# Gated linear attention of a hybrid decoder layer: tiles turned by VectorE and DMA instead of TensorE, and the order of three queues written out

## Chip, cores, metric

One core of a Trainium2 chip. The metric is the device time of one launch in microseconds, taken as the median of the runs; beside it stands one profiled execution, whose trace is read below. An engine's queue runs its instructions in order; the five engines wait for one another through semaphores.

## What is computed

One layer of a hybrid decoder, for a prompt of 2048 tokens and for 64 sampled tokens (8 sequences of 8). D is 1024, the feed-forward width 4096, everything in float32. Cut to what matters here:

```
h    = rms_norm(x, g_mix_pre)
proj = h @ w_in            # -> q, k, v (window attention) | gq, gk, gv, gr, glr (GLA)
attn = sliding-window attention with sinks, rotary, 8 q heads, 2 kv heads, hd 64
log_a = log_sigmoid(glr @ w_gk2 + b_gk) / 16
# GLA: 4 heads, dk 64, dv 128
S_t = exp(log_a_t) * S_{t-1} + k_t v_t^T          # state, 64 x 128 for each head
o_t = (q_t / 8) S_t
o   = rms_norm(o, g_gla) * silu(gr)
mix = concat(attn, o) @ w_out
x   = x + rms_norm(mix, g_mix_post)
x   = x + rms_norm(relu(rms_norm(x) @ w_up)^2 @ w_down, g_ffn_post)
```

Outputs are both streams, the last 128 keys and values, and the GLA states.

## The kernel before

The prompt is 16 tiles of 128 tokens (i = 0 to 15); the sampled tokens are a seventeenth (NB). The stages follow one another: window attention, GLA, output projection, feed-forward (up, then down). Float32 products are made of three products of rounded halves (high by high, high by low, low by high). This document is about the GLA stage, from about 308 to 675 us of the trace.

**Fill.** The loop over the tiles (L1545) runs the generator `gla(i)`. Wherever `gla` yields a number n, the loop emits n products from the generator `fill`: the input projection of later tiles (`projecting`, tile `gproj`, 96 products of 128x384 for one tile of tokens in four chunks of columns), and at the end the first output projections (128x512). So TensorE's queue is written out by hand (`te` is an `InOrder`, which ties each instruction to the one before it on that engine): pieces of `gla`, and between them so many products. The numbers are G_FILL, G_FIRST_FILL and, inside `finish_out`, 44. ScalarE copies each finished chunk out of PSUM into `gp` (L656, two buffers, one for each tile of tokens).

**gla(i).** Queries and keys come out of the projection with tokens on partitions; the products within a tile need them with features on partitions. `qk_T` (L1106) turns four 128x128 squares on TensorE (tile `gqk`), VectorE copies the keys to `kt` (L1114), ScalarE the two halves of the queries to `qz` (L1116). The decays are worked into seven levels of a tree: `level_sums` (L1150) makes, at each level, exponentials of two running sums (ScalarE) and two sums (VectorE); `weighted` (L1129) multiplies them into keys (XK) and queries (XQ). `keys_decayed` (L1137) makes the keys for the state's update and turns them back, two squares on TensorE (tile `kdT`, in the same bank as the turn of the ranks, L1145). Then the products of the levels (tiles `gl`, `gh`), of the update (`ds`) and with the old state (`o`, `ds`), from which `put_level` (L1162) picks masked parts into AH; ScalarE and VectorE make AT of it, and four products of AT with the values finish the output. `finish_out` (L1178) squares, takes a power on GpSimd, scales by the gate, turns four squares on TensorE (tile `ogT`) and stores them (`mo`, L1207, L1208) as rows 4 to 7 of `mix_d`, from which the output projection loads its left operand (L1392). `decayed(i + 1)` and the level sums 0 to 2 of the next tile stand ahead of the level products of this one.

**Order.** TensorE's order is laid down. VectorE, ScalarE and SyncE take the GLA stage's work as a planner places it; some instructions are tied by `issue_after`. Between tiles, two generators share the stage: `sampled` (the seventeenth tile's GLA) during the first tiles and then `split_wo` (L1438), which loads the eight slices of w_out, splits each (ScalarE and VectorE, 128x1024) and stores the parts, one slice for each tile.

Of the kernel before, what the change touches and what calls it, by code (L numbers as in the profile page):

```python
# [12 lines left out]
F32 = mybir.dt.float32  # L13
# [62 lines left out]
G_FILL = (34, 14, 16, 8, 20)  # L76
G_FIRST_FILL = 66
# [75 lines left out]
def hybrid_step_kernel(ctx: ExitStack, tc: tile.TileContext, I, O):  # L153
# [19 lines left out]
    te, ac, dv = (InOrder(tc, engine) for engine in (nc.tensor, nc.scalar, nc.vector))  # L173
# [22 lines left out]
    wo_d = [dpool.tile([P, 2, D], F32, name=f"wo_d{k}") for k in range(KT)]  # L196
    sm_d = dpool.tile([P, NFC, 2, 2 * NS], F32, name="sm_d")
# [427 lines left out]
    def load_T(i, xT):  # L625
        for u in range(2):
            dst = xT[1][:, :, u * NS : (u + 1) * NS] if i == NB else xT[u]
            nc.sync.dma_start(f32(dst), xt_d[i][:, u])
        return xT
# [346 lines left out]
    def log_decays(i, z, t, gt, out):  # L976
        for g in range(2):
            te.matmul(z[:, g], wgk[:, i % 2, g * P : (g + 1) * P], gt[:, : z.shape[2]], start=True, stop=True)
        nc.scalar.activation(t, z, AF.Abs)
        nc.scalar.activation(t, t, AF.Exp, scale=-1.0)  # L980
        if out is not None:
            nc.scalar.activation(out, t, AF.Ln, bias=1.0)
        return z
# [54 lines left out]
    ogs, mos = places("og", [P, 4, P]), places("mo", [P, 4, P])  # L1038
    XK = sp.tile([P, NL, 2, P], F32, name="XK")
    XQ = sp.tile([P, NL, 2, 2, P // 2], F32, name="XQ")  # L1040
    sgs, prs = places("sg", [P, 512]), places("pr", [P, 256])
# [3 lines left out]
    kts = places("kt", [P, 2, P], 2)  # L1045
# [29 lines left out]
    def decays(i, n, before, kind="d"):  # L1075
# [7 lines left out]
        if i:  # L1083
# [5 lines left out]
        nc.vector.scalar_tensor_tensor(before, z, 0.0, t, op0=ALU.min, op1=ALU.subtract)  # L1089

    def gate(i, gp, n):

        gr = gp[:n, 1024:1536]
        t = next(sgs) if n == P else s_sg
        nc.scalar.activation(t[:n], gr, AF.Abs)
        nc.scalar.activation(t[:n], t[:n], AF.Exp, scale=-1.0)
        nc.scalar.activation(t[:n], t[:n], AF.Ln, bias=1.0)
        nc.vector.scalar_tensor_tensor(t[:n], gr, 0.0, t[:n], op0=ALU.min, op1=ALU.subtract)
        nc.scalar.activation(t[:n], t[:n], AF.Exp)
        engine = nc.vector if i in (0, NB) else nc.gpsimd  # L1100
# [3 lines left out]
        return t  # L1104

    def qk_T(i, gp, n, kind="d"):  # L1106
# [6 lines left out]
        kt, q = (next(kts), qz) if n == P else (s_kt, s_qz)  # L1113
        nc.vector.tensor_copy(kt, pt[:, :, 0, :])  # L1114
        for r, rr in enumerate(half_of):
            nc.scalar.activation(q[rr, r], pt[rr, :, 1, :], AF.Copy, scale=0.125)  # L1116
        return kt
# [11 lines left out]
    def weighted(xk, xq, dec, kt, q, l, b):  # L1129

        dl, dr = (pairs(dec[:, l], b, s) for s in range(2))
        if l:
            nc.vector.tensor_tensor(pairs(xk[:, l], b, 0), dl, pairs(kt, b, 0), op=ALU.mult)
        out = xq[:, l].rearrange("p r g (m b) -> p r (g m) b", b=b)
        nc.vector.tensor_tensor(out, dr.unsqueeze(1).to_broadcast(list(out.shape)), pairs(q, b, 1), op=ALU.mult)

    def keys_decayed(after, kt, kdT, n, kind, kd, pair=0):  # L1137

        nc.scalar.activation(kdT, after, AF.Exp, scale=1.0 / 16)
        nc.vector.tensor_tensor(kdT, kdT, kt, op=ALU.mult)  # L1140
        yield
        pk = bank([P, 3, P], kind, f"kdT_{n}")
        for g in range(2):
            te.transpose(pk[:n, g, :], kdT[:, g, :], ident)
        ranks = ranks_T(pair, pk[:, 2]) if pair else None  # L1145
        nc.scalar.activation(kd[:n], pk[:n, :2].rearrange("p g k -> p (g k)"), AF.Copy)
        if pair:
            nc.scalar.activation(glrT[pair % 2], ranks, AF.Copy)

    def level_sums(before, after, dec, l, b):  # L1150

        left, right = halves(dec[:, l], b)
        (bl, br), al = halves(before, b), halves(after, b)[0]
        nc.scalar.activation(right, br, AF.Exp, scale=1.0 / 16)
        if l:
            nc.scalar.activation(left, al, AF.Exp, scale=1.0 / 16)
        nc.vector.tensor_tensor(al, al, br[..., b - 1 :].to_broadcast(list(al.shape)), op=ALU.add)
        nc.vector.tensor_tensor(br, br, bl[..., b - 1 :].to_broadcast(list(br.shape)), op=ALU.add)  # L1160

    def put_level(at, gm, mk, b):  # L1162
# [3 lines left out]
        nc.vector.copy_predicated(dst, m, gm.rearrange("p h (m b) -> p h m b", b=b))  # L1166

    def put_diagonal(i, at, gp, n):

        pr = next(prs)  # L1170
        with tc.issue_after(put[0].ins) if 0 < i < NB else nullcontext():
            nc.vector.scalar_tensor_tensor(pr[:n], gp[:n, 0:256], 0.125, gp[:n, 256:512], op0=ALU.mult, op1=ALU.mult)
        dg = sp.tile([P, 4], F32, tag="dg", name=f"dg_{i}", bufs=2)
        nc.vector.tensor_reduce(dg[:n], pr[:n].rearrange("p (h d) -> p h d", h=4), op=ALU.add, axis=AX.X)
        shape = [n, 4, HD]
        nc.vector.copy_predicated(at, dmsk[:n].unsqueeze(1).to_broadcast(shape), dg[:n].unsqueeze(2).to_broadcast(shape))

    def finish_out(i, og_src, sg, n, kind):  # L1178

        ssq = sp.tile([P, 4], F32, tag="ossq", name=f"ossq_{i}", bufs=2)  # L1180
        junk = sp.tile([P, P], mybir.dt.bfloat16, tag="ojunk", name=f"ojunk_{i}", bufs=1)
        for h in range(4):
            nc.scalar.activation(junk[:n], og_src(h), AF.Square, accum_out=ssq[:n, h : h + 1])
        rs = sp.tile([P, 4], F32, tag="ors", name=f"ors_{i}", bufs=2)
        rsqrt_mean(sp, rs[:n], ssq[:n], n, P, 4)
# [4 lines left out]
        for h in range(4):  # L1190
            with tc.issue_after(put[0].ins) if i == NB else nullcontext():
                nc.vector.scalar_tensor_tensor(
                    og[:n, h, :], og_src(h), rs[:n, h : h + 1], sg[:n, h * P : (h + 1) * P],
                    op0=ALU.mult, op1=ALU.mult,
                )
        for _ in range(S_WAIT[0] if i == NB else 1):
            yield 44, True
# [3 lines left out]
        if i == NB - 1:  # L1201
            hi, lo = late_mix
            nc.vector.tensor_copy(hi, pt)
            nc.vector.tensor_tensor(lo, pt, f32(hi), op=ALU.subtract)
        else:
            mo = next(mos)
            nc.scalar.activation(mo[:, :, :n], pt[:, :, :n], AF.Copy)  # L1207
            nc.sync.dma_start(mix_d[i][:, 4:8, :], mo[:, :, :n])  # L1208

    def decayed(i):  # L1210

        before, after = next(befores), next(afters)
        yield from decays(i, P, before, "d" if i else "b")
# [3 lines left out]
    def gla(i, gp, og=iter(())):  # L1217
# [4 lines left out]
        before, after = pre.pop(i)  # L1222
        next(og, None)
        kt = qk_T(i, gp, P, "c")
        dec = next(decs)
        following = decayed(i + 1) if i < NB - 1 else iter(())
        yield G_FILL[0] + 3 * (i == 1) if i else G_FIRST_FILL, True
        deque(og, 0)
        put_diagonal(i, AH, gp, P)
        for l, b in enumerate(LEVELS):  # L1230
            if l < 3 or i == 0:
                level_sums(before, after, dec, l, b)
            else:
                with tc.issue_after(put[0].ins):
                    level_sums(before, after, dec, l, b)
            if l == NL - 1:
                kd = next(kds)
                pair = i // 2 + 1 if i % 2 == 0 and i < NB - 2 else 0
                turned = keys_decayed(after, kt, next(kdTs), P, "e", kd, pair)
                nc.scalar.activation(dec[:, NL], before, AF.Exp, scale=1.0 / 16)  # L1240
            weighted(XK, XQ, dec, kt, qz, l, b)
        next(turned)
# [1209 lines left out]
```

## Time and profile before

| | |
|---|---|
| median of 3 runs | 2150.69 us (2150.44 to 2151.86) |
| the profiled execution | 2150.7 us, of it the span of the trace 2148.9 us |
| granted TensorE clock | 0.999 of full speed |
| TensorE busy | 99% of the span |
| VectorE, ScalarE, GpSimd busy | 71%, 57%, 12% |
| moved by DMA | 411.55 MB in 241323 packets |

Busy time of TensorE is modelled from pipelined instructions, each of which lasts longer than the distance to the next. How long a piece of its queue takes is therefore read from the start of the piece to the start of what follows it. The "mean ns" of an instruction of the other engines is its own duration; neighbours can overlap by some tens of ns.

### The profile page before, as it was taken

The page shows a single profiled execution, that of the slowest core. Times are in us where ns is not written, and L with a number is a line of the kernel's source. Part 1 is how long each engine was busy: PE and PEld are TensorE (multiplying, and loading weights), DVE is VectorE, ACT ScalarE, POOL GpSimd, SP SyncE. Part 2 cuts the span into 40 slices and gives each one's busy share as a digit, 9 for nine tenths or more (in the row PEclk, how much of TensorE's full clock was granted, in tenths as well). Part 3 has the DMA queues.
Part 4 walks back from the last instruction along what each step waited for, and adds up shares of the span by engine and source line. Part 5 has one row for each costly group of instructions (what it writes and reads, how often), then busy time and mean ns, then how long its engine had stood idle before and what let it go on. Part 6 is the DMA issues. An engine that isn't in the chain of part 4 may idle for free.

```text
span 2148.9 us, 34602 instructions
## 1 busy us (share of the span) xinstructions
PE 2137.8 (99%) x11974; PEld 1853.1 (86%) x11974; DVE 1530.2 (71%) x3200; ACT 1215.7 (57%) x2627; POOL 261.7 (12%) x422
## 2 busy tenths in 40 slices
PE   9999999999999999999999999999999999999998
PEld 9999999999998888888888888888888888888887
DVE  7999868778875666988887555557776666555566
ACT  7999867566664444655555544345444445544454
POOL 4676511111211110000000000000000000000000
PEclk9999999999999999999999999999999999999999
DMA  7444341243437567777886777668544443766685
GB/s 244 157 145 149 100 118 46 85 144 117 154 112 259 186 221 240 250 261 266 264 276 219 257 240 225 211 201 274 172 171 162 152 161 121 261 202 193 194 274 176
DMA packets 241323, 411.55 MB, mean 192 GB/s; under 512 B 24876, under 2 KB 143132, under 8 KB 237036
## 3 DMA queue, kind: packets, MB, share of 16 engines
q1 hardware_dynamic: 240988, 409.08, 57.6%
q8 instruction: 94, 1.54, 0.3%
q14 instruction: 81, 0.66, 0.1%
q10 hardware_dynamic: 160, 0.27, 0.0%
HBM read 265.82 MB, written 143.99 MB: 191 GB/s over the span
## 4 chain that ended last, share of the span: by engine, by line
PE 92%; DVE 3%; ACT 2%; DMA 1%; issue 1%; POOL 0%; SPq 0%; DVEq 0%; ACTq 0%; POOLq 0%
PE dn L142 28%; PE gproj L142 11%; PE uc L142 8%; PE uX L142 8%; PE out L1432 7%; PE proj L142 6%; PE ue L142 4%; PE ud L142 4%; PE ub L142 4%; PE dsam L142 1%; PE sc L142 1%; PE pT L142 1%; PE sam L142 1%; PE av L142 1%; PE out L142 1%
## 5 line engine op out<-in xcount | busy, mean ns | idle before, releaser
L142 PE MATMUL dn<-o0t,o0s 128*128 128x512 f32 x888 | 345.4, 389 | 0.6 <-DVE f L2090 0.6
L142 PE MATMUL dn<-o1t,o0s 128*128 128x512 f32 x888 | 345.7, 389 | 0.0
L142 PE MATMUL dn<-o0t,o1s 128*128 128x512 f32 x888 | 345.6, 389 | 0.0
L2076 DVE TENSOR_TENSOR o1s<-rs,o0s 128x512 fp32r<-128x512 f32 x224 | 154.5, 691 | 221.5 <-ACT o0s L2075 219.2
L2075 ACT ACTIVATE o0s<-rs 128x512 fp32r<-128x512 f32 x224 | 141.2, 631 | 291.4 <-PE dn L142 255.6
L142 PE MATMUL gproj<-wg,gxh 128*128 128x384 f32 x1024 | 271.1, 341 | 0.0
L142 PEld LDWEIGHTS dn<-o0t,o0s 128*128 128x128 f32 x888 | 166.8, 188 | 37.1 <-DVE f L2090 1.0
L142 ACT ACTIVATE st<-st 128x512 f32<-128x512 f32 x224 | 141.1, 630 | 100.5 <-DVE st L142 95.6
L142 PEld LDWEIGHTS dn<-o1t,o0s 128*128 128x128 f32 x888 | 166.7, 188 | 35.6 <-DVE o1t L2076 0.3
L142 PEld LDWEIGHTS dn<-o0t,o1s 128*128 128x128 f32 x888 | 166.7, 188 | 34.6
L142 PE MATMUL uc<-H,s 128*128 128x512 f32 x768 | 186.5, 391 | 0.1
L142 PEld LDWEIGHTS gproj<-wg,gxh 128*128 128x128 f32 x1024 | 183.8, 188 | 2.4 <-issue 1.9
L142 PE MATMUL gproj<-wg,gxl 128*128 128x384 f32 x576 | 185.9, 340 | 0.0
L142 PE MATMUL uX<-H,w 128*128 128x512 f32 x768 | 185.3, 390 | 0.0
L142 PEld LDWEIGHTS uX<-H,w 128*128 128x128 f32 x768 | 144.0, 188 | 30.4
L142 PEld LDWEIGHTS uc<-H,s 128*128 128x128 f32 x768 | 143.0, 188 | 30.6 <-ACT st L142 0.3
L1432 PE MATMUL out<-wo,mt 128*128 128x512 f32 x680 | 158.6, 392 | 0.0
L218 POOL TENSOR_TENSOR frs<-rs_v,half 128x1 f32<-128x1 f32 (+1 forms) x13 | 12.2, 944 | 1198.5 <-DVE rs_v L216 1198.5
L2076 DVE TENSOR_TENSOR o1t<-rt,o0t 128x512 fp32r<-128x512 f32 x222 | 151.9, 685 | 4.8 <-ACT o0t L2075 4.8
L1432 PEld LDWEIGHTS out<-wo,mt 128*128 128x128 f32 x680 | 126.5, 188 | 26.1
L2075 ACT ACTIVATE o0t<-rt 128x512 fp32r<-128x512 f32 x222 | 137.0, 619 | 8.8 <-DMA rt<-t_d 6.6
L142 DVE TENSOR_TENSOR st<-st 128x512 f32<-128x512 f32 x160 | 110.6, 692 | 31.4 <-ACT st L142 27.1
(444 smaller groups left out, 4314.8 us busy)
## 6 DMA issues: line engine op xcount, KB each, us to landing
s_d<-st SPq DMA_DIRECT2D x32, 1792.0 KB, 8.3
rs<-s_d SPq DMA_DIRECT2D x224, 256.0 KB, 3.6
raw<-in_w_up SPq DMA_DIRECT2D x64, 512.0 KB, 5.0
rt<-t_d SPq DMA_DIRECT2D x128, 256.0 KB, 3.9
rt<-in_w_down SPq DMA_DIRECT2D x96, 256.0 KB, 3.2
t<-in_w_down SPq DMA_DIRECT2D x64, 256.0 KB, 3.8
t_d<-t SPq DMA_DIRECT2D x32, 512.0 KB, 5.5
h_d<-ht SPq DMA_DIRECT2D x8, 1280.0 KB, 7.9
```

The source lines that it names most:

```text
L142: ins = call(*a, **k)
L218: return nc.gpsimd.tensor_tensor(out, v[:n], e, op=ALU.pow)
L1432: te.matmul(banks[c], x, w[:, c * 512 : (c + 1) * 512], start=k + u == 0, stop=k == KT - 1 and u == len(products) - 1,)
L2075: high = nc.scalar.activation(hi, raw, AF.Copy)
L2076: low = nc.vector.tensor_tensor(lo, raw, f32(hi), op=ALU.subtract)
```

## The change

The turns of tiles leave TensorE, except in the first and the last tile. Where a square was turned there, VectorE now turns 32x32 blocks (`transpose`), and DMAs through a buffer in device memory put the blocks in their places, in runs of 32 numbers (128 bytes). Queries and keys of tile i + 1 are turned while tile i is worked on (`turn`), so the projection must be that much further ahead; `qkT` has two buffers. The decayed keys are turned by `keys_turn`. The output is turned by VectorE alone within blocks, stored by four DMAs in a layout of its own (`gm_d`), and `fetch_mix` puts the blocks in place when the output projection loads them: five DMAs where one was. VectorE, ScalarE and SyncE are `InOrder` in this stage (`dv`, `ac`, `sq`), so the order of the program is that of the queues. The work of a tile is cut into six parts with fills (14, 20, 14, 18, 8, 20); the two sums of the last level, whose results only `kdT` and the last decay needed, are replaced by a bias in the exponential (`whole`, with `edge`).

```diff
-G_FILL = (34, 14, 16, 8, 20)
-G_FIRST_FILL = 66
+G_FILL = (14, 20, 14, 18, 8, 20)
+G_LAST_FILL = (11, 15, 11, 12, 6, 15)
+G_FIRST_FILL = (10, 50)
...
-    te, ac, dv = (InOrder(tc, engine) for engine in (nc.tensor, nc.scalar, nc.vector))
+    te, ac, dv, sq = (InOrder(tc, engine) for engine in (nc.tensor, nc.scalar, nc.vector, nc.sync))
...
+    qk_d = {i: dpool.tile([4, 4, 32, P], F32, name=f"qk_d{i}") for i in range(1, NB - 1)}
+    kd_d = [dpool.tile([4, 4, 32, HD], F32, name=f"kd_d{i}") for i in range(NB - 1)]
+    gm_d = [dpool.tile([32, 16, 4, 32], F32, name=f"gm_d{i}") for i in range(NB - 1)]
...
+    def turn(i, gp):
+
+        qkT = qkTs_of[i] = next(qkTs)
+        dv.transpose(
+            blocks.rearrange("t (a u x) -> t u a x", a=4, u=4), gp[:, :512].rearrange("x (u a t) -> x u a t", u=4, a=4)
+        )
+        for c in range(4):
+            src = blocks[c * 32 : c * 32 + 32].rearrange("t (a e) -> t a e", a=4)
+            sq.dma_start(qk_d[i][c].rearrange("a t e -> t a e"), src)
+        for u in (2, 3, 0, 1):
+            src = qk_d[i][..., u * 32 : u * 32 + 32].rearrange("c a t x -> (a t) c x")
+            sq.dma_start(qkT[:, u // 2, u % 2].rearrange("p (c x) -> p c x", c=4), src)
...
+    def keys_turn(i, kdT, kd):
+
+        dv.transpose(
+            blocks[:, :256].rearrange("x (c g t) -> x g c t", c=4, g=2), kdT.rearrange("t g (c x) -> t g c x", c=4)
+        )
+        for a in range(4):
+            src = blocks[a * 32 : a * 32 + 32, :256].rearrange("x (c e) -> x c e", c=4)
+            sq.dma_start(kd_d[i][a].rearrange("c x e -> x c e"), src)
+        for g in range(2):
+            src = kd_d[i][..., g * 32 : g * 32 + 32].rearrange("a c x t -> (c x) a t")
+            sq.dma_start(kd[:, g * P : (g + 1) * P].rearrange("p (a t) -> p a t", a=4), src)
+
+    def whole(out, t, u):
+
+        src, outs = halves(t, 64), halves(out, 64)
+        ac.activation(outs[1 - u], src[1 - u], AF.Exp, scale=1.0 / 16)
+        for g in range(2):
+            ac.activation(outs[u][:, g], src[u][:, g], AF.Exp, bias=edge[:, g, 1 - u : 2 - u], scale=1.0 / 16)
...
+        if i < NB - 1:
+            yield
+            mo = next(mos)
+            dv.transpose(mo.rearrange("t a h x -> t h a x"), og.rearrange("x h (a t) -> x h a t", a=4))
+            for c in range(4):
+                src = mo[c * 32 : c * 32 + 32].rearrange("t a h x -> t (a h) x")
+                out_stores.append(lambda c=c, src=src: sq.dma_start(gm_d[i][:, :, c, :], src))
+            return
...
+        take(x_loads, 1)
+        diagonal = put_diagonal(i, AH, gp, P)
+        if i == 0:
+            deque(first_sums(before, after, dec), 0)
+        for l, b in enumerate(LEVELS[3:6], 3):
+            next(diagonal, None)
+            level_sums(before, after, dec, l, b)
+        for l in (1, 2, 3):
+            weighted_keys(XK, dec, kt, l, LEVELS[l], dv)
+        ac.activation(edge, before[:, :, HD - 1 :: HD], AF.Copy, scale=1.0 / 16)
+        whole(kdT, after, 0)
+        for r, rr in enumerate(half_of):
+            ac.activation(qz[rr, r], qkT[rr, 0], AF.Copy, scale=0.125)
+        dv.tensor_tensor(kdT, kdT, kt, op=ALU.mult)
+        if i < NB - 1:
+            keys_turn(i, kdT, kd)
+        take(x_loads, 1)
+        yield fills[0], False
         next(og, None)
...
+        level_sums(before, after, dec, NL - 1, LEVELS[-1])
+        whole(dec[:, NL], before, 1)
+        for l in (4, 5):
+            weighted_keys(XK, dec, kt, l, LEVELS[l], dv)
+        for l, b in enumerate(LEVELS[:6]):
+            if l == 3:
+                next(og, None)
+            weighted_queries(XQ, dec, qz, l, b, dv)
+        next(og, None)
+        weighted_keys(XK, dec, kt, 6, LEVELS[6], dv)
+        weighted_queries(XQ, dec, qz, 6, LEVELS[6], dv)
+        next(og, None)
+        if i < NB - 1:
+            take(out_stores)
+        yield fills[1] + 2 * (i == 1), True
...
+        next(following, None)
+        sg = next(sgs)
+        gating = gate(i, gp, P, sg)
+        yield fills[2], True
+        assert {(i, c) for c in range(4)} <= projected
+        next(gating)
+        if i + 1 < NB - 1:
+            assert {(i + 1, 0), (i + 1, 1)} <= projected
+            turn(i + 1, gps[i + 1])
+        qd = next(qds)
+        dv.scalar_tensor_tensor(qd, qkT[:, 0], 0.125, dec[:, NL], op0=ALU.mult, op1=ALU.mult)
         deque(following, 0)
...
+        sums = first_sums(*pre[i + 1], dec) if i < NB - 1 else iter(())
+        for part in (sums, gating, sums, gating, sums):
+            next(part, None)
+        deque(sums, 0)
+        take(put_off)
+        yield fills[3], True
+        yield fills[4], True
...
+    def fetch_mix(i, raw, ks, queue):
+        n = rows(i)
+        if i >= NB - 1:
+            placing[:] = [queue.dma_start(raw[:, :ks, :n], mix_d[i][:, :ks])]
+            return
+        queue.dma_start(raw[:, :4], mix_d[i][:, :4])
+        for a in range(4):
+            src = gm_d[i][:, 4 * a : 4 * a + 4].rearrange("t h c x -> t (h c x)")
+            placing[:] = [queue.dma_start(raw[a * 32 : a * 32 + 32, 4:].rearrange("t h e -> t (h e)"), src)]
```

What follows the last `yield` shown (the products of the levels, `put_level`, AT, the state, a fill of 20, the products of AT, `next(wo_parts)`) keeps its place, on `dv` and `ac`. The loads of the next tile's projection operand (`x_loads`) are issued at the two `take(x_loads, 1)`, and the loads and stores of w_out's parts (`put_off`) at `take(put_off)`.

More of the change, by code (lines that the diff above doesn't have):

```diff
@@ L1222, in gla @@
         before, after = pre.pop(i)
-        next(og, None)
[L1224 to L1241, printed above, removed]
@@ L1242, in gla @@
[L1242 to L1252 removed]
+        ends = i in (0, NB - 1)
+        fills = G_LAST_FILL if i == NB - 1 else G_FILL if i else G_FIRST_FILL + G_FILL[2:]
@@ new lines, in gla @@
+        if ends:
+            qkTs_of[i] = next(qkTs)
+            qk_T(i, gp, P, "c")
+        qkT = qkTs_of.pop(i)
+        kt = qkT[:, 1]
+        dec, kd, kdT = next(decs), next(kds), next(kdTs)
+        following = decayed(i + 1) if i < NB - 1 else iter(())
+        take(x_loads, 1)
[4 more added lines that the diff above has]
+            next(diagonal, None)
+            level_sums(before, after, dec, l, b)
```

247 lines of the change are left out of this document (140 added, 107 removed).

## Prediction

> **What bounds the kernel now.** I read the page's busy line, then the busy time in windows of one tile of the GLA stage each, then the chain of waits, then TensorE's timeline.
>
> ```profile
> span 2148.9 us, 34602 instructions
> 486.79:508.07 21.28, 21.28 (x190) 20.62 (x189) 17.23 (x52) 14.26 (x43) 4.03 (x4) 1.00 0.41 137
> sum 127.64, PE 127.33 PEld 122.67 DVE 103.94 ACT 85.93 POOL 24.21; mean PE 21.22 PEld 20.44 DVE 17.32 ACT 14.32 POOL 4.03
> 486.86 1.08 PE gl L142 x32
> 508.14 1.08 PE gl L142 x32
> ```
>
> The second line is one tile: its length, then busy us of TensorE, weight loads, VectorE, ScalarE, GpSimd, the granted clock, DMA's share and GB/s. The third sums six such tiles (465 to 615 us): TensorE is busy in 127.33 of 127.64 us, VectorE in 17.32 of 21.27 on average. The chain of waits goes through TensorE's level products at 486.86 and 508.14, a period of 21.28 us. TensorE sets the end; other engines count only if they come to need more than the new period, or if a wait of theirs is on TensorE's path.
>
> ```profile
> 490.73 0.51 PE L142 MATMUL gproj<-wg,gxh 128*128 128x384 f32 x2
> 491.25 0.51 PE L142 MATMUL gproj<-wg,gxh 128*128 128x384 f32 x2
> 494.05 0.60 PE L142 MATMUL gqk<-ident,gp 128*128 128x128 f32 x4
> 494.40 0.42 PE L142 MATMUL gproj<-wg,gxl 128*128 128x384 f32 x1
> 500.39 0.60 PE L142 MATMUL ogT<-ident,og 128*128 128x128 f32 x4
> 500.74 0.42 PE L142 MATMUL z<-glrT,wgk 128*128 128x128 f32 x2
> 484.90 0.34 PE L142 MATMUL gproj<-wg,gxh 128*128 128x384 f32 x1
> 485.08 0.38 PE L142 MATMUL kdT<-ident,kdT 128*128 128x128 f32 x2
> 485.48 0.34 PE L142 MATMUL gproj<-wg,gxl 128*128 128x384 f32 x1
> ```
>
> **The change part by part. TensorE.** Start to start: three fill products take 0.52 us (490.73 to 491.25), 0.173 each. The turn of queries and keys takes 494.40 - 494.05 = 0.35 us, that of the output 500.74 - 500.39 = 0.35. Around the turn of the decayed keys, 484.90 to 485.48 holds two fill products and the turn: 0.58 - 0.35 = 0.23. `qk_T` goes in tiles 1 to 14, the other two in 0 to 14: 14 x 0.35 + 15 x 0.35 + 15 x 0.23 = 4.9 + 5.25 + 3.45 = **13.6 us**. The turn of the ranks only moves into the bank of `z`. The fill is the same products in another division. So the ideal is 2150.7 (the profiled execution, of which 2148.9 are the span; the median, 2150.69, is the same) - 13.6 = 2137.1, a period of 21.28 - 0.93 = 20.35. All else is what can take this back.
>
> ```profile
> L1160 DVE TENSOR_TENSOR before<-before 128x128 f32<-128x128 f32 x112 | 41.7, 372 | 8.0 <-ACT gp L656 0.5 <-ACT dec L1158 0.5 <-ACT dec L1156 0.4
> L1159 DVE TENSOR_TENSOR after<-after,before 128x128 f32<-128x128 f32 x112 | 36.3, 324 | 8.7 <-ACT dec L1158 1.9 <-POOL after L1214 0.4
> L1114 DVE COPY kt<-gqk 128x256 f32<-128x256 f32 x16 | 6.7, 418 | 0.1
> L1249 DVE TENSOR_TENSOR qd<-qz,dec 64x256 f32<-64x256 f32 x32 | 13.3, 417 | 0.3
> L1098 DVE SCALAR_TENSOR_TENSOR sg<-gp,sg 128x512 f32<-128x512 f32 x16 | 11.0, 685 | 0.7 <-ACT sg L1097 0.6
> L229 DVE TENSOR_TENSOR wop<-wor,wop 128x1024 fp32r<-128x1024 f32 x8 | 9.8, 1226 | 0.9
> 505.30 1.24 DVE L1160 TENSOR_TENSOR before<-before 128x128 f32<-128x128 f32 x1
> 505.10 1.29 POOL L1103 TENSOR_TENSOR sg<-sg,ggla 128x512 f32<-128x512 f32 x1
> ```
>
> **VectorE** loses, for each tile, the copy of the keys (0.418), the two sums of the last level (0.372 + 0.324) and one of two `qd` (0.417): 1.53 us. It gains three transposes, of 512, 256 and 512 numbers a partition, which the trace doesn't show. By the nearest rows, a 512-wide instruction at 0.685 and a 256-wide one at 0.418, they cost 2 x 0.685 + 0.418 = 1.79. The low end is half of that, 0.9; for the high end I take twice, 3.6, since one row shows a sum growing from 0.28 to 1.24 us beside a GpSimd product. So 17.32 - 1.53 + 1.79 = **17.6 us** of 20.35, between 16.7 and 19.4; I take 17.6 because the moved bytes of the transposes are those of these rows. VectorE stays below the period, with less room than before (2.8 us for 4.0). [...]
>
> ```profile
> L1207 ACT ACTIVATE mo<-ogT 128x512 f32<-128x512 f32 x15 | 8.8, 584 | 0.5 <-PE ogT L142 0.5
> L1146 ACT ACTIVATE kd<-kdT 128x256 f32<-128x256 f32 x16 | 5.9, 371 | 2.8 <-PE kdT L142 2.7
> L1139 ACT ACTIVATE kdT<-after 128x256 f32<-128x256 f32 x16 | 6.6, 415 | 0.7 <-DVE after L1159 0.5
> L1287 ACT ACTIVATE AT<-gh 64x128 f32<-64x128 f32 x32 | 8.7, 272 | 36.6 <-DVE AH L1166 36.4
> ```
>
> **ScalarE** loses two copies (0.584 + 0.371) and two 256-wide exponentials (0.415 each); `whole` adds six narrower ones, `edge` a seventh, at about 0.27 to 0.31 each as the 0.272 row: -1.79 + 2.0 = +0.2, so 14.5 of 20.35. Since its queue is now in program order, a wait of `qz` on its DMA holds up the copies of finished chunks behind it, and these free TensorE's banks: see the round trip.
>
> ```profile
> q1 hardware_dynamic: 2372, 1.18, 82.0%
> 304.17 1.06 SPq L628 DMA_DIRECT2D gxl<-xt_d  x2
> q1 hardware_dynamic: 288, 1.05, 39.4%
> q1 hardware_dynamic: 864, 2.88, 40.8%
> mix_d<-mo SPq DMA_DIRECT2D x15, 256.0 KB, 2.0
> ```
>
> **DMA.** Before, a tile's transfers are runs of 2 to 4 KB. New for each tile: turning queries and keys writes 512 runs of 512 bytes and reads 2048 of 128; keys write 512 of 256 and read 1024 of 128; the output writes 2048 of 128. That is 6144, in 18 issues; with 16 completion packets for each, 6432. The price comes from 304 to 310 us (first line), where two loads of the sampled tile move 2048 runs of 256 bytes: 2372 packets took 0.82 x 16 x 6 = 78.7 us of engine time, 33 ns each, the high end. Without the 128 packets of 4 KB in it, which by the load at 400 to 408 us cost 0.394 x 16 x 8 / 256 = 197 ns each (third line), it is (78.7 - 25.2) / 2244 = 24 ns; this I take, half of it being the low end (128 bytes, not 256). So 6432 x 24 / 16 = 9.6 us of all engines for each tile. In the eight tiles that also move a slice of w_out, the traffic before is 0.408 x 21.3 = 8.7 us (fourth line, 486.8 to 508.1): 18.3 of 20.35, nearly full but below. In the other tiles it is far below.
>
> **The round trip** is the new wait. In order of the program, VectorE turns tile i + 1, SyncE issues four writes, waits for them to land, issues four reads; `kt` and `qz` of the next tile wait for these. Queued behind a late one are: on SyncE the decayed keys' round trip and the next operand's load, on VectorE everything to the end of the tile, on ScalarE the chunk copies. Length: issues at 0.53 each (two in 1.06) are 2.1 us, landing 2.0 (last line of the fence), the 2048 reads at 24 ns / 16 = 3.1 and landing again 2.0, with VectorE's 0.7: **about 10 us**, between 8 (issues at 0.32, a row further down) and 11.5 (33 ns). Room: from the use of `kt` to the next turn VectorE has three key products, `kdT`, its transpose, the other products, the output's scaling and transpose:
>
> ```profile
> L1133 DVE TENSOR_TENSOR XK<-dec,kt 128x128 f32<-128x128 f32 x96 | 23.5, 285 | 0.1
> L1135 DVE TENSOR_TENSOR XQ<-dec,qz 128x256 f32<-128x256 f32 x112 | 41.1, 419 | 0.7 <-ACT qz L1116 0.6
> L1192 DVE SCALAR_TENSOR_TENSOR og<-o,ors,sg 128x128 f32<-128x128 f32 x32 | 11.1, 347 | 12.4 <-POOL ors L218 12.4
> ```
>
> The sum is 6 x 0.285 + 7 x 0.419 + 4 x 0.347 + 0.42 + 0.42 + 0.69 = 7.6 us. Turn to turn must fit 20.35, so the trip may last 12.7. It fits, with some 3 us of room. The decayed keys have a shorter trip (1024 reads), and TensorE has 74 products, 12.8 us, between the place where they are turned and their use.
>
> **Output projection.** Five loads for one add four issues, 1.3 to 2.1 us, ahead of the split of the next tile's operand:
>
> ```profile
> 721.84 0.32 SPq L1392 DMA_DIRECT2D mt<-mix_d  x1
> 726.56 1.06 ACT L228 ACTIVATE mt<-mt 128x1024 fp32r<-128x1024 f32 x1 [3.05 <-DMA mt<-mix_d]
> 728.52 1.22 DVE L229 TENSOR_TENSOR mt<-mt 128x1024 fp32r<-128x1024 f32 x1
> 734.25 0.95 PE L1432 MATMUL out<-wo,mt 128*128 128x512 f32 x3
> ```
>
> The split ends at 729.74, its first product starts at 734.25: 4.5 us of cover, so nothing; without it, up to 2 us for each of 13 tiles.
>
> **What I add.** The last tile has 96 products of fill left where there were 122, so less stands over its chain: 0 to 2 us, I take 1. The eight w_out tiles also hold VectorE's 1.226 (it is in the 17.23 of such a tile) with DMA nine tenths full: 0 to 4 us, I take 1. Forecast: 2137.1 + 2 = **2139 us**, on its own between 2135.5 and 2143.
>
> **The rivals.** *The round trip is late (slower).* At one place: `kt` at the head of a tile. It decides from 12.7 us on; each us beyond costs 14 (tiles 1 to 14). At 14 us: 2139 + 1.3 x 14 = 2157; it is as before at 13.5. For it: nearly full DMA queues in the w_out tiles, SyncE in order, and runs of 128 bytes written to memory, for which no row exists. Against: 24 ns measured at 256. [...]
>
> *DMA becomes the bound in the w_out tiles.* At 33 ns a run, 13.3 + 8.7 = 22.0 us for a tile: 1.65 over, eight times, 13 us, and the gain is gone: 2151.
>
> *VectorE becomes the bound.* At 19.4 us, plus the waits in its order for GpSimd's power and the logarithm (0.90 and 0.69 in one tile):
>
> ```profile
> 497.90 0.35 DVE L1192 SCALAR_TENSOR_TENSOR og<-o,ors,sg 128x128 f32<-128x128 f32 x1 [0.90 <-POOL ors L218]
> 504.37 0.42 DVE L1089 SCALAR_TENSOR_TENSOR before<-z,zt 128x256 f32<-128x256 f32 x1 [0.69 <-ACT zt L982]
> ```
>
> the period is 21.0, a gain of 0.28 x 14 = 4: 2147. That the change doesn't do what it says would look the same: turns gone from TensorE, its queue as long as before because it idles.
>
> **How the numbers follow.** Forecast 0.62, late round trip 0.13, DMA 0.13, VectorE or an idling TensorE 0.12. This kernel can be told from no change at about 0.2%, 4.3 us: below 2146.4 is faster, above 2155.0 slower. Faster: the forecast, half of the VectorE case, and the mild ends of the other two: 0.71. Slower: most of the late trip and the worst of DMA: 0.14. Same: 0.15. The range 2135 to 2154 takes in VectorE's case, the DMA case and a trip up to 13.8 us.
>
> **What would show it.** Right: level products 20.3 to 20.6 us apart in tiles 3 to 13, no `gqk` and `ogT` in them, TensorE without idle time; transposes of 0.6 to 0.8 us at 512; VectorE near 17.6 us a tile; reads of `qkT` landed before VectorE's first `XK`. Wrong: VectorE or ScalarE waiting for `qkT` at the head of each tile (round trip); DMA shares above 0.95 and a longer period in tiles 4 to 11 only (DMA); transposes above 1.2 us and VectorE busy in all of the period (VectorE). The forecast fails if TensorE idles before the level products or at full banks.

## The result and the profile after

| | before | after |
|---|---|---|
| median | 2150.68 us (2150.44 to 2151.86) | 2201.81 us (2201.24 to 2205.62) |
| ratio | | 1.024, 95% interval 1.0223 to 1.0258 |
| span of the profiled execution | 2148.9 us | 2200.0 us |

The changed kernel is 51 us slower, where 12 us faster was forecast. Two tiles of the changed kernel in windows from level products to level products come first (columns as in the prediction: length; busy us of TensorE, weight loads, VectorE, ScalarE, GpSimd; granted clock; DMA share; GB/s).

```profile
535.52:555.94 20.42, 20.42 (x182) 19.83 (x181) 15.50 (x47) 12.55 (x41) 1.37 (x2) 1.00 0.54 144
582.98:605.26 22.28, 20.68 (x181) 19.77 (x180) 16.58 (x50) 14.01 (x45) 1.97 (x4) 1.00 0.57 153
sum 66.85, PE 62.05 PEld 59.31 DVE 51.97 ACT 41.40 POOL 8.55; mean PE 20.68 PEld 19.77 DVE 17.32 ACT 13.80 POOL 2.85
```

The first tile has the period that was forecast, 20.42 for 20.35 us. It is the only one among 15. The second has the length that comes most often, 22.3 us, in four of the 15: TensorE has its work done in 20.68 us and idles the rest. The third line sums three such tiles (583 to 605, 631 to 675 us). Nine others take 21.1 to 32.7 us, and the last 34.6. TensorE idles 1.6 us in each of the three, though VectorE, ScalarE and GpSimd are all busy for less than the period.

What TensorE waits for, from the view of its waits over the GLA stage and the start of the output projection (total us, times, longest), first before, then after:

```profile
PE ds L142 <- ACT kd L1146: 0.9, 2, 0.6
```

```profile
PE gproj L143 <- ACT gp L143: 18.5, 6, 9.4
PE z L143 <- ACT zt L143: 17.7, 7, 4.8
PE out L143 <- ACT mt L1520: 9.0, 2, 7.6
PE o L143 <- DVE S L143: 1.8, 2, 1.3
```

These four rows are 47.0 us against 0.9. `gproj<-ACT gp` is a fill product whose PSUM bank ScalarE has not yet copied out. `z<-ACT zt` is the turn of the ranks, which waits until ScalarE's Abs has read the bank it shares with `z`. `out<-ACT mt` is the output projection's first operand, split late. None of these rows names a transfer. Along the stage: the level products of tile 0 start 11.6 us later than before (338.77 for 327.23), those of the last tile 50.3 us later (709.95 for 659.67).

The operations that had no row before the change, from the groups of instructions (count, busy us, mean ns) and the DMA issues (KB each, median us from issue to landing):

```profile
L143 DVE STREAM_TRANSPOSE mo<-og 128x512 f32<-128x512 f32 x15 | 10.6, 705 | 0.0
L143 DVE STREAM_TRANSPOSE blocks<-gp 128x512 f32<-128x512 f32 x14 | 9.6, 683 | 2.8 <-ACT gp L143 2.4 <-DMA kd_d<-blocks 0.4
L143 DVE STREAM_TRANSPOSE blocks<-kdT 128x256 f32<-128x256 f32 x15 | 6.7, 445 | 0.5
```

```profile
qkT<-qk_d SPq DMA_DIRECT2D x56, 64.0 KB, 2.0
kd<-kd_d SPq DMA_DIRECT2D x30, 64.0 KB, 2.2
gm_d<-mo SPq DMA_DIRECT2D x60, 64.0 KB, 3.4
```

The prices of the transposes were right: 0.70, 0.68 and 0.45 us. The reads in runs of 128 bytes land in 2.0 and 2.2 us, as the store of 256 KB did before (2.0); the output's writes in such runs take 3.4.

### The profile page after: what moved, and what is told of

It is laid out like the page before. It is cut to its first block, busy times and chain, and to the rows that moved or that the text cites. A ratio compares the mean times of both kernels' runs of the same rounds, so it can differ in the third digit from the quotient of the medians.

```text
span 2200.0 us, 34683 instructions
## 1 busy us (share of the span) xinstructions
PE 2139.9 (97%) x11828; PEld 1849.8 (84%) x11828; DVE 1550.3 (70%) x3182; ACT 1216.7 (55%) x2679; POOL 258.8 (12%) x422
## 4 chain that ended last, share of the span: by engine, by line
PE 81%; DVE 6%; ACT 6%; DMA 4%; issue 2%; SPq 1%; POOL 1%; DVEq 0%; ACTq 0%; POOLq 0%
PE dn L143 27%; PE uc L143 8%; PE uX L143 8%; PE proj L143 6%; PE out L1552 5%; PE gproj L143 5%; PE ue L143 4%; PE ud L143 4%; PE ub L143 4%; PE dsam L143 1%; PE sam L143 1%; PE sc L143 1%; ACT dec L143 1%; PE pT L143 1%; PE av L143 1%
## 5 line engine op out<-in xcount | busy, mean ns | idle before, releaser
L143 PE MATMUL gproj<-wg,gxh 128*128 128x384 f32 x1024 | 276.2, 347 | 9.1 <-ACT gp L143 9.1
L143 PE MATMUL gproj<-wg,gxl 128*128 128x384 f32 x576 | 191.2, 351 | 9.4 <-ACT gp L143 9.4
L143 PEld LDWEIGHTS gproj<-wg,gxh 128*128 128x128 f32 x1024 | 188.8, 193 | 13.7 <-ACT gp L143 11.1
```

The lines of the kernel that those rows point to most:

```text
L143: ins = call(*a, **k)
```

## The experiments

Three theories were held against each other: 1, TensorE waits for a ScalarE whose queue, in the order of the program, lags; 2, the round trips or SyncE's written order cause it; 3, VectorE has no room. The ratios below stand against medians of 2149.5 to 2150.7 us of the kernel before, timed beside each group.

| run | what it is | median us | ratio to before (95%) |
|---|---|---|---|
| e1 | ranks turned ahead of z | 2193.2 | 1.0203 (1.0188 to 1.0218) |
| e2 | chunk copies placed by the planner | 2235.5 | 1.0400 (1.0385 to 1.0416) |
| e3 | both, and both ends | 2236.7 | 1.0405 (1.0390 to 1.0421) |
| e4 | written order undone | 2175.9 | 1.0124 (1.0107 to 1.0141) |
| e5 | order kept, turns undone | 2273.9 | 1.0573 (1.0556 to 1.0589) |
| e6 | less of VectorE | 2200.6 | 1.0235 (1.0218 to 1.0251) |
| e7 | no round trips | 2196.3 | 1.0213 (1.0197 to 1.0229) |
| e8 | e1, VectorE's half of the split later | 2185.7 | 1.0165 (1.0147 to 1.0183) |
| e9 | e4, ranks first | 2170.3 | 1.0095 (1.0079 to 1.0110) |
| e10 | e1, ScalarE's half of the split earlier | 2169.1 | 1.0095 (1.0078 to 1.0112) |
| e11 | e10, gate on VectorE | 2161.4 | 1.0052 (1.0037 to 1.0066) |
| e12 | e9, SyncE in written order | 2195.4 | 1.0209 (1.0194 to 1.0225) |
| e13 | e11, tile 0 mended | 2158.4 | 1.0041 (1.0027 to 1.0055) |
| e14 | e13, last tile mended | 2159.0 | 1.0042 (1.0029 to 1.0054) |
| e15 | e13, operand loads first in tile 0 | 2158.3 | 1.0039 (1.0025 to 1.0052) |

### One wait at a time: e1, e2, e3

```diff
# e1
+            ranks = ranks_T(pair, pz[:, 2]) if pair else None
             z = log_decays(i, pz[:, :2], t, gt, t)
             if pair:
-                ac.activation(glrT[pair % 2], ranks_T(pair, pz[:, 2]), AF.Copy)
+                ac.activation(glrT[pair % 2], ranks, AF.Copy)
# e2
-                columns = projecting(i, xT[i], (c,), nc.scalar if i == NB else ac)
+                columns = projecting(i, xT[i], (c,), nc.scalar)
```

> Changed kernel with one edit: in the tiles where the ranks are turned in the bank of z, TensorE turns them ahead of the two products of z, not behind them, so the turn no longer waits until ScalarE's Abs has read the bank. Theory 1 (the loss is TensorE waiting for a ScalarE queue that lags): the seven waits z<-ACT zt (17.7 us together in the changed kernel) go, with the half-clock stretches behind them (about 6 us): 2202 - 18 to 24 = 2178 to 2186, if the lag doesn't come out at another wait of TensorE. Rival 2 (late DMA round trips): no change, 2198 to 2206. Rival 3 (VectorE has no room): the waits move to other tiles, 2195 to 2206.

> Changed kernel with one edit: ScalarE's copies of finished chunks out of PSUM are no longer tied into its written order; the planner places them, as before the change. Theory 1: the six waits gproj<-ACT gp (18.5 us) go with their half-clock stretches (about 8 us); the waits at z stay: 2202 - 20 to 27 = 2175 to 2182. Rival 2 (DMA): no change beyond 0.2%. Rival 3 (VectorE): TensorE's waits stay near 48 us in sum, under other names.

> Changed kernel with the ranks turned first, the chunk copies and the splits of w_out's slices placed by the planner, tile 0's memset of `after` on VectorE, and the loads of the output projection's first operands issued before the loads of w_out's parts. The turns by VectorE and DMA stay whole. Theory 1: nearly all of the 48 us of waits and 16 us of half clock go: 2138 to 2150, so the turns off TensorE are worth their 13.6 us. Rivals 2 and 3: the DMA trips and VectorE's work are all still there, so above 2185.

e1 gained 8.6 us of the 18 to 24, e2 lost 33.7, e3 34.9. TensorE's waits in e1:

```profile
PE gproj L143 <- ACT gp L143: 29.3, 12, 9.4
```

The waits at `z` are gone, and 10.8 us of them came back at the chunk copies, 12 times for 6. In e2, the waits of TensorE, then ScalarE's own (393 to 650 us):

```profile
PE z L143 <- ACT zt L143: 28.3, 7, 6.2
PE o L143 <- DVE S L143: 11.6, 8, 2.6
```

```profile
ACT gp L660 <- PE gproj L143: 51.1, 20, 4.4
```

The planner set the copies early in ScalarE's queue, where they stood 51.1 us for chunks that TensorE had not finished (5.6 us in the changed kernel), and all that is in written order stood behind them. So the first form of theory 1, that each wait can be taken away by itself, fell: something slower than TensorE sets the pace, and shows at whichever place TensorE meets it next.

### Which part costs: e4, e5, e6, e7

```diff
# e4
+    ac, dv, sq = nc.scalar, nc.vector, nc.sync
# e5
-        ends = i in (0, NB - 1)
+        ends = True
...
-            turn(i + 1, gps[i + 1])
...
-            keys_turn(i, kdT, kd)
+        keys_T(kdT, P, "e", kd)
# e6
-            weighted_queries(XQ, dec, qz, l, b, dv)
+            if l > 2 or i == 0:
+                weighted_queries(XQ, dec, qz, l, b, dv)
# e7
-            sq.dma_start(qkT[:, u // 2, u % 2].rearrange("p (c x) -> p c x", c=4), src)
...
+        if i > 1:
+            return
```

> Changed kernel with the written order of VectorE, ScalarE and SyncE taken away in the GLA stage (the planner places their work; TensorE's order stays; the turns by VectorE and DMA stay, and the turn of the ranks stays behind z). Theory 1: the copies come earlier, Abs may too; most of the 48 us go: 2145 to 2175. If the turns themselves cost the time (rivals 2 and 3): above 2190, since they are all still there.

> Changed kernel with the turns taken back: queries and keys, decayed keys and output are turned by TensorE in every tile and copied by VectorE and ScalarE, nothing goes through device memory, the output projection loads one operand as before; the written order of the three queues, the cut into six parts and the fills stay. TensorE's own work is that of before, 13.6 us more. Theory 1b (after the first four runs: in the written order ScalarE and VectorE wait for each other in turn, a loop of some 22 us a tile, over TensorE's 20.35; taking one of TensorE's waits away only lets the lag come out at the next): the loop is there without the turns too, only 1.4 us of VectorE shorter, and TensorE still waits: 2160 to 2190. Rivals 2 and 3 (the trips, or the transposes, cost the time): as before, 2146 to 2156.

> Changed kernel that leaves out the products of the decays with the queries at levels 0 to 2 in tiles 1 to 15 (three instructions of 0.42 us on VectorE, 1.26 us a tile); nothing else is left out. Theory 1b: the loop through VectorE gets 1.26 us a tile shorter, of which TensorE's waits give back nearly all: 2202 - 14 to 19 = 2183 to 2188. Rival 2 (DMA trips, SyncE): no change, 2196 to 2204, since the trips start where they did. Rival 1 (only ScalarE's lag): no change either.

> Changed kernel that leaves out the DMAs of the turned queries and keys (tiles 2 to 14 use tile 0's) and, from tile 2 on, those of the decayed keys; VectorE's transposes stay, and so do the output's stores. Rival 2 (round trips, or SyncE's order, hold up ScalarE and VectorE): most of the loss goes, 2145 to 2165. Theory 1b: only the wait for one slice of w_out (3.8 us on ScalarE) and what it led to goes: 2190 to 2200.

With all turns kept and only the written order gone, e4 recovers half of the loss, 26 of 51 us, and ends at the edge of its range. e7 takes the trips of queries, keys and decayed keys away and recovers 5.5, within its range: as a price of the trips, theory 2 fell for all but that. SyncE's written order stays in e7. e6 takes 1.26 us a tile from VectorE and changes nothing (2200.6 for 2201.8): theory 3 fell, and so did the form of theory 1 (1b in the expectations) that put the loop through VectorE's sum of work. e5 is slower still, far above its range, but not a clean price of the order: TensorE waited 61.2 us in it at the turn of the output,

```profile
PE ogT L143 <- DVE og L143: 61.2, 15, 5.2
```

a place in TensorE's order that was chosen for this run.

### The ring: e8, e10

e1's last tiles are evenly spaced at 22.28 us. Tiles of the same length are in the changed kernel and in e6, so without e6's products too. The chain of waits of e1 through one of them (start, us, what):

```profile
645.97 1.08 PE gl L143 x32
...
648.78 3.33 PE gproj L143 x18
...
652.61 1.06 ACT wop L143
...
653.82 1.01 issue
654.83 0.42 DVE blocks L143
...
655.81 0.52 ACT dec L143 x2
...
659.09 0.31 ACT qz L143
...
661.54 1.07 ACT dec L143 x5
662.61 0.48 ACT gp L143
...
663.13 5.13 PE gproj L143 x28
668.26 1.08 PE gl L143 x32
```

TensorE ends a chunk at 652.11 (648.78 + 3.33) and ScalarE copies it. Then ScalarE's order has the split of a slice of w_out (`wop`), for which VectorE waits; the sums and exponentials of levels 3 to 5, in turn with VectorE (655.81 on); `qz`; the squares; five exponentials; and only at 662.61 the next copy. The program gives the chunks two banks, that is two chunks of 24 products at 0.173 us, 8.3, and some 1 us of other products. Here 10.5 us lie between the copies, so TensorE waits, runs 28 products, and reaches the level products at 668.26. The four stretches, 6.1 to the chunk's end, 10.5 to the next copy, 0.5 for it and 5.1 to the level products, are the 22.3 us. Each engine is idle for part of the ring, so none looks like a bound.

e8 moves VectorE's half of the split out of the way, e10 ScalarE's half to a place where ScalarE waits anyway and leaves VectorE's where it was. Both load the output projection's first operands earlier, e10 also the first two slices of w_out.

```diff
# e8
-            dv.tensor_tensor(parts[1], raws[k], f32(parts[0]), op=ALU.subtract)
+            late.append(lambda k=k, parts=parts: dv.tensor_tensor(parts[1], raws[k], f32(parts[0]), op=ALU.subtract))
...
             keys_turn(i, kdT, kd)
+        take(late)
# e10, in gla, behind the next tile's first sums
         take(put_off)
+        take(halves_due)    # ac.activation(parts_of[k][0], raws[k], AF.Copy)
         yield fills[3], True
```

> Changed kernel with the ranks turned first, the first operands of the output projection loaded earlier, and VectorE's half of the split of a slice of w_out (wop) put into its order a third of a tile later, behind the transpose of the decayed keys, where ScalarE's half is long done; order and turns else as they are. Theory 1b: VectorE's wait for ScalarE's half (16.9 us over seven tiles in the changed kernel) leaves the loop, and the last tile's 9 us shrink: 2193 (ranks first alone) - 12 to 25 = 2168 to 2181. Rival 2: 2185 to 2195.

> Changed kernel with ranks first and earlier operand loads (as in e8), and ScalarE's half of the split of a slice of w_out moved in its order to the place behind the next tile's first sums, where ScalarE waits 4.3 us for VectorE, so that it no longer stands between two copies of chunks; VectorE's half keeps its place. Theory 1c (a ring: chunk's end, copy, 11 us of ScalarE and VectorE in turn, next copy, 5 us of products, level products, chunk's end, measured 22.28 us in e1's tiles 11 to 14 whatever VectorE's load): the split's 1.05 us on ScalarE and VectorE's wait of 1.0 leave the ring; tiles 11 to 14 come to 20.4 to 21.5 us, the kernel to 2168 to 2182 (e8: 2185.7). If ScalarE's order is not what counts there: 22.3 us as before and 2184 or more.

e8 fell short of its range (2185.7 for 2168 to 2181), and its last tiles took 22.60 us: ScalarE's half still stood in the ring, and TensorE now waited for VectorE's state as well (`o<-DVE S`, up to 1.1 us in these tiles). e10 came where the ring puts it, 16.6 us below e8. Level products of e1, then of e10, two tiles each:

```profile
623.62 0.45 PE L143 MATMUL gl<-XQ,qkT 128*64 128x64 f32 x8
645.90 0.45 PE L143 MATMUL gl<-XQ,qkT 128*64 128x64 f32 x8
```

```profile
606.69 0.45 PE L143 MATMUL gl<-XQ,qkT 128*64 128x64 f32 x8
627.30 0.45 PE L143 MATMUL gl<-XQ,qkT 128*64 128x64 f32 x8
```

22.28 us there, 20.61 here, for an edit that leaves every engine the same work.

### Contention of VectorE and GpSimd: e11

A stretch of the changed kernel's timeline (start, us, engine, operation), GpSimd's two products of the gate and VectorE's sums of level 2:

```profile
461.70 1.28 POOL L1118 TENSOR_TENSOR sg<-sg,gp 128x512 f32<-128x512 f32 x1 [5.50 <-ACT sg L143]
462.07 1.05 DVE L143 TENSOR_TENSOR after<-after,before 128x128 f32<-128x128 f32 x1 [0.57 <-ACT dec L143]
463.06 1.27 POOL L1120 TENSOR_TENSOR sg<-sg,ggla 128x512 f32<-128x512 f32 x1
463.16 1.31 DVE L143 TENSOR_TENSOR before<-before 128x128 f32<-128x128 f32 x1
```

Each of VectorE's sums ends just after the product beside which it runs: 463.12 after 462.98, 464.47 after 464.33. In the written order they meet in each of 13 tiles (391 to 679 us), and on the way to `put_level`: two sums take 1.04 to 1.34 us there, where the same sums at 468 to 472 us, with no product beside them, take 0.29. What holds the sums is not shown by these rows; what a kernel without GpSimd's two products gains is asked in e11.

```diff
-        engine = vector if i in (0, NB) else nc.gpsimd
+        engine = vector
```

> The kernel of e10 with the two products of the output's gate on VectorE (2 x 0.69 us more of it) in place of GpSimd. In the changed kernel two of VectorE's sums in each tile take 1.05 and 1.33 us, beside GpSimd's products, where others take 0.30. If that contention lengthens the ring: 0.4 us a tile less net, 3 to 8 us below e10. If VectorE's sum of work is what counts (rival 3): 10 to 20 us above e10.

VectorE gets two products of 0.69 us more in each tile, and the kernel is 7.7 us faster. The sums by groups, e10, then e11 (460 to 640 us):

```profile
L143 DVE TENSOR_TENSOR before<-before 128x128 f32<-128x128 f32 x52 | 24.5, 470 | 2.4
L143 DVE TENSOR_TENSOR after<-after,before 128x128 f32<-128x128 f32 x52 | 22.0, 423 | 10.9 <-ACT dec L143 10.1
```

```profile
L143 DVE TENSOR_TENSOR before<-before 128x128 f32<-128x128 f32 x53 | 15.5, 293 | 2.9 <-ACT dec L143 0.5
L143 DVE TENSOR_TENSOR after<-after,before 128x128 f32<-128x128 f32 x53 | 15.4, 291 | 8.1 <-ACT dec L143 7.2
```

Over tiles 4 to 13, VectorE is busy for 18.3 us a tile in e10 and 17.8 in e11, though it does more. In e10 no engine waits for the gate's products between 460 and 640 us, so a late gate does not explain the gain. ScalarE's waits for `put_level`'s AH fall from 31.1 to 17.3 us in that stretch. Two tiles of e11 in windows:

```profile
599.02:619.43 20.41, 20.41 (x181) 19.82 (x180) 17.53 (x53) 13.84 (x44) 1.37 (x2) 1.00 0.67 174
619.43:639.85 20.42, 20.42 (x182) 19.82 (x181) 17.34 (x51) 14.10 (x45) 1.37 (x2) 1.00 0.49 115
```

From tile 5 to tile 14, e11 takes 20.41 to 20.55 us a tile without a wait of TensorE. That is the forecast's period, with the turns by VectorE and DMA whole.

### The planner instead: e9, e12

```diff
# e9: e4, e1's edit, and the first operands' loads earlier; e12: the same, with
-    ac, dv, sq = nc.scalar, nc.vector, nc.sync
+    ac, dv = nc.scalar, nc.vector
```

> The kernel of e4 (written order of VectorE, ScalarE and SyncE taken away in the stage) with the ranks turned ahead of z and the first operands of the output projection loaded earlier. Theory 1b (TensorE waits for what stands late in the written queues; where the planner places the work, single places are left): the waits z<-ACT zt (8.5 us in e4) go and those at the output projection (5.8) shrink: 2176 - 8 to 14 = 2162 to 2168. If the turn of the ranks were only a place at which a general lag shows, as after the chunk copies in e1: 2172 to 2176.

> As e9, but SyncE keeps its written order; only VectorE and ScalarE are placed by the planner. In e4 TensorE waited 7.8 us for the decayed keys' reads (ds<-DMA kd), which the planner had issued late. Theory: these go, and 2153 to 2162 is left. If SyncE's written order is part of the loss (rival 2): above e9.

e9 gained 5.6 us, less than forecast; 7.3 us of waits for the decayed keys' reads are left. e12 is 25 us slower than e9, the opposite of what was hoped: it was to take away the waits for the decayed keys' reads. TensorE's waits for them in e9, then in e12, and SyncE's longest wait in e12 (393 to 650 us):

```profile
PE ds L143 <- DMA kd<-kd_d: 7.3, 5, 2.9
```

```profile
PE ds L143 <- DMA kd<-kd_d: 11.8, 11, 3.9
```

```profile
SPq L143 <- DVE blocks L1186: 56.0, 9, 12.0
```

SyncE keeps its order while the planner puts VectorE's transposes later, and all other transfers queue behind them. In tiles 5 to 14 the transpose of the decayed keys starts 18 to 26 us behind the level products that precede it in e12, 10 to 22 in e9 and 10 to 12 in e11. SyncE's wait alone does not tell the runs apart: the same one is 71.3 us long in the changed kernel and 39.0 in e9. So here a queue in written order behind one that is placed otherwise cost more than both free. This is what is left of theory 2; how the 25 us divide was not settled.

### Both ends: e13, e14, e15

```diff
# e13
+        if i == 0:
+            yield 30, False
...
-        nc.gpsimd.memset(after, 0.0)
+        (nc.gpsimd if i else nc.vector).memset(after, 0.0)
# e14, ahead of the last tile's work
+            for m in placed_first:
+                mixes[m[0]] = split_mix(*m, put)
# e15, e13 and in tile 0
             take(x_loads)
+            keys_turn(i, kdT, kd)
```

> The kernel of e11 with tile 0 mended: 30 of its 60 first products stand ahead of its level sums in the order (so their chunk's copy does too), and its memset of `after` is on VectorE. In e11 the level products of tile 0 start 10.7 us later than before the change (one wait of 9.4 us, gproj<-ACT gp). If that wait is the price of the written order at one place: it goes, 2161.4 - 8 to 11 = 2150 to 2153, level products of tile 0 near 328 us. If the chain of tile 0 itself is late: the wait comes out at the level products, 2156 to 2161.

> The kernel of e13 with the split of the output projection's first two operands written into ScalarE's and VectorE's order ahead of the last tile's work. In e11 TensorE waits 6.2 us there (out<-ACT mt, out<-DVE mt); 2 to 4 of them go: 2147 to 2150, if the loads have landed by then; if they land late, ScalarE's last tile is held up and it is 2152 to 2158. The whole theory says that a version with all such places mended comes to 2137 plus what is left in TensorE's waits.

> The kernel of e13 with one move in tile 0: SyncE issues the loads of the next operand ahead of the trip of the decayed keys, behind which they stood. In e13 the wait gproj<-ACT gp of tile 0 was gone, but TensorE waited 3.8 us for these loads (gproj<-DMA gxh) in its place, and the level products of tile 0 started at 333.7 us (before the change 327.2). If SyncE's written order is what is late there: they start at 328 to 330 us, and the kernel comes to 2153 to 2156. If ScalarE's and VectorE's chain of tile 0 is just behind: 332 us or later, and 2157 to 2160.

All three are short of the ranges that were hoped for, and in each another wait came in the place of the one removed. e13's tile 0 lost the 9.4 us wait and got another, the next operand's load behind the decayed keys' trip on SyncE; e15 moved that, its level products start at 329.05 us as forecast, and a third wait appeared behind them, so its time is e13's. The rows of e13, then of e15:

```profile
PE gproj L143 <- DMA gxh<-xt_d: 3.8, 1, 3.8
```

```profile
PE o L143 <- DVE S L143: 3.9, 1, 3.9
```

In e14 the waits for the split of the first operands went, and 3.7 us of waits for the loads of w_out's parts took their place, with the DMA engines 0.96 to 1.05 busy there. So no version beat the kernel before, and none reached the forecast: the best are 8.2 to 8.5 us above the kernel before. Where this lies can be read from e15's level products, compared with those before the change (7.3 us between the two profiled executions). Those of tile 0 start 1.8 us later; the way from them to tile 1 is 5.9 us longer (27.5 for 21.5), that from tile 2 to 3 is 1.7 longer, the last one 5.3 (28.8 for 23.5), and what follows the last 1.9. The other twelve are 9.4 us shorter together. Part of the 5.9 is the wait of 3.9 above; part of the 5.3 are waits for the output projection's first operand, 3.8 in sum. What would remove them is open.

## Why the prediction was wrong

**The step that failed** is ScalarE's: "14.5 of 20.35. Since its queue is now in program order, a wait of `qz` on its DMA holds up the copies of finished chunks behind it, and these free TensorE's banks: see the round trip." That late copies would leave TensorE without a free bank was right, and the list of what would make the forecast fail even names full banks. But only a late DMA was taken as a cause, and ScalarE and VectorE were judged by busy time against the period. What counts is the distance between two copies in ScalarE's written order, with every turn it takes with VectorE in it. e1's chain shows 10.5 us where two banks give about 9.3, in a queue that is busy for 14 of 22. With that distance shortened (e10, e11) the period is as forecast. Step by step: the ranks first gave 8.6 us (e1), ScalarE's half of the split with the earlier loads 24.1 (e10), the gate on VectorE 7.7 (e11) and tile 0 3.1 (e13), some 43 of the 51 together.

**TensorE's saving** was right: 20.41 us in e11 and 20.42 in one tile of the changed kernel, for 20.35. It holds for the tiles in the middle; over the whole kernel no run shows the 13.6 us.

**"The turn of the ranks only moves into the bank of `z`"**, costed at nothing, was wrong: it shows 17.7 us of waits, the longest 4.8, since the bank is read by ScalarE later. It was worth 8.6 us (e1), as the ring took the rest.

**VectorE** came within its range: 18.3 us a tile over tiles 4 to 13 of the changed kernel (441 to 675 us) and 17.8 in e11, for 17.6. The 17.3 of the three tiles above leaves out the longer ones between them. The transposes took 0.68 to 0.71 and 0.45, 1.8 us a tile in sum, for the 1.79 forecast. As a rival (VectorE the bound by its busy time) it was wrong: e6. The price of GpSimd's contention was in a row of the prediction (1.24 us), taken only as a bound for the transposes and not looked for on the path; moving the gate away was worth 7.7 us (e11).

**DMA** was priced too high. The tile with a slice of w_out shown above has a share of 0.57 x 22.28 = 12.7 us, those of e11 13.0 to 15.0, for the 18.3 forecast. Over tiles 4 to 13 the changed kernel's share is 0.55 of 234.4 us and that of before 0.38 of 213.8, 12.9 and 8.1 us a tile. That is 4.8 us for 6432 packets, some 12 ns each, not 24.

**The round trip** was right: no wait of VectorE or ScalarE for `qkT` shows in the stage, and e7 gives 5.5 us for the trips. The last read is issued 5.9 to 10.8 us behind the start of the transpose; with 2.0 for its landing, that is 8 to 13 us for the 10 forecast.

**"What I add"**, 1 us for the last tile, was mis-sized: the last interval of the changed kernel took 34.6 us (675.39 to 709.95) for 23.5 before. Tile 0, in which nothing was expected, lost 11.6.

Of the rivals none came true as told. The remark that turns could be gone "from TensorE, its queue as long as before because it idles" describes the trace, though it was given to VectorE's busy time.

## What to carry to other kernels

When a queue that a planner filled is put in program order, look for what frees another engine's buffers in it, and add up everything between two such instructions, waits for the other engines included; compare this with what the buffers cover, not the engine's busy time with the period. If a wait is taken away and its time comes back under another name, look for a ring of several engines with the same period in tile after tile, and shorten that. Putting one queue in order and leaving those it waits for free can be worse than leaving all of them free (e12, 25 us above e9).

## What the runs showed of the hardware

TensorE's granted clock fell to 0.50 at each of the changed kernel's seven waits of 2.92 to 9.40 us between 300 and 760 us; in the kernel before it is 0.99 or more in every stretch of 2 us in which TensorE works. The end of tile 0's wait (timeline), and windows over it:

```profile
322.87 8.06 PE L143 MATMUL gproj<-wg,gxl 128*128 128x384 f32 x30 [9.40 <-ACT gp L143]
```

```profile
316.00:320.00 4.00, 0.00 (x0) 0.00 (x0) 2.83 (x10) 1.86 (x8) 0.00 (x0) 0.78 0.00 0
320.00:324.00 4.00, 1.13 (x4) 1.13 (x5) 3.59 (x13) 3.37 (x13) 0.31 (x1) 0.50 0.09 17
324.00:328.00 4.00, 4.00 (x14) 4.00 (x14) 2.06 (x6) 0.36 (x1) 0.00 (x0) 0.50 0.36 58
328.00:332.00 4.00, 3.53 (x21) 3.39 (x20) 0.88 (x2) 1.91 (x4) 0.00 (x0) 0.94 0.89 244
```

The granted clock is 0.50 from within the wait to some 5.6 us behind its end, so 30 products took 8.06 us that take 5.2 at 0.173: this wait of 9.40 us cost some 2.8 us more than its length. The measured 51 us are the saving of 13.6 taken from about 65, of which the waits' rows above hold 47. Most of the rest is such stretches: TensorE's busy time from 300 to 760 us, in windows of 0.5 us, times what the granted clock lacked of 1, gives an estimated 16 us. Shorter waits did it too. Behind the wait of 2.92 us for `zt` that ends at 527.0 us:

```profile
526.00:528.00 2.00, 1.00 (x4) 1.00 (x5) 1.77 (x7) 1.94 (x9) 1.26 (x2) 0.62 0.12 21
528.00:530.00 2.00, 2.00 (x8) 2.00 (x7) 2.00 (x6) 1.94 (x5) 0.00 (x0) 0.53 0.88 209
```

The three waits of 1.6 us at chunk copies, ending at 599.2, 647.7 and 670.3 us, left the clock at 1.00. Of two waits of nearly the same length, one of 2.52 us in e5 (ending at 482.54 us) had products of 0.32 us each behind it (484.49 to 485.45), one of 2.51 in e10 (403.12) had them at 0.173 (403.58 to 404.10). Within the wait of 9.40 us the clock was still 1.00 up to 318 us, 4.5 us after its start, and 0.50 from 318.5; within that of 2.92 it was 0.98 from 526.0 to 526.5, 2.4 us after its start, and 0.50 from there. From which length on a wait lowers the clock, these traces do not settle.
